# Returned rows read on the queue of the weights, the first tile behind the last weights; gate chunks split behind the last pair's scatters

## The chip, the cores and the metric

One core of a Trainium2 chip runs the kernel. The metric is the device time of one execution in microseconds (us). It has five engines that work side by side and wait for one another by semaphores: TensorE (PE in the profile; its weight loads are PEld), VectorE (DVE), ScalarE (ACT), GpSimd (POOL) and SyncE (SP). SP issues most DMAs here. DMAs issued by SP, ACT and POOL are carried out by the same 16 DMA engines.

## The reference, cut to what matters

One decoder layer over 512 tokens of width 1024, in float32. Everything up to the router is untouched; what counts here is the end of it.

```python
h = h + mix @ w_out
h = h + hier_moe(rmsnorm(h, norm2_g), ...)      # 32 gated-MLP experts, top 2 of one group
gate = sigmoid(rmsnorm(h, ple_norm_g) @ ple_gate_w + ple_gate_b)
e = p @ ple_proj_w
h = h + gate * e
return rmsnorm(h, final_norm_g)
```

## The kernel before, in words

**Experts.** The 32 experts run as 16 pairs (`for i in range(16)`, L1165). For a pair, `gate_up` (L991) multiplies 128 gathered rows (64 slots for each expert) by the gate and up weights, and `down` (L1014) by the down weights. The weights come as 96 units of 1 MB (`load_units`, L685) on SP, of which three are under way at a time: each waits for the one three before it. For pairs 0 to 14 the result is scattered to a table `yd` in device memory by an indirect DMA of POOL (L1043). The last pair doesn't go through memory: `down(15)` splits its result into a high part (`oh`, ACT, L1038) and a low part (`ol`, DVE, L1039), and `scatter` (L1046) adds it to the residual `h1` by matmuls with a one-hot matrix: two matmuls and one DVE addition for each of four token tiles and each half (hf) of the 1024 columns.

**Returned rows.** A tile t of 128 tokens gets back the two rows per token that the experts 0 to 14 of its choice left in `yd`: `load_y(t)` (L1160) reads them, 1 MB, into a buffer `ys[t]`, and `add_y(t)` (L1155) adds the two to `h1[t]`, one DVE instruction each. Since the rows come out of `yd`, the read must wait until the last scatter has landed. All four reads stand on POOL's queue, behind the last scatter.

**The gate matrix.** It comes in four loads of 1 MB (`gate_load`, L1058), on SP behind the last weights, then two rows of constants (`rows`). Each of its eight chunks k of 128 rows, in two halves of 512 columns, is split for the matmul (`split_gate`, L1062): ACT writes the rounded high part scaled by the norm's gain (L1068), DVE the low part (L1069). That makes 16 splits. In the code before, three stand in `down(15)` ahead of the high part of its result, one behind the first tile's scatters, and twelve behind `turn(0)`.

**The end.** `turn(t, hf)` (L1207) transposes half a tile on PE and copies it (ACT) and its rest (DVE). `ple(n)` (L739) runs n matmul steps of the embedding product `e` (PE, L724), which ACT takes out of PSUM (L735); the last twelve steps, three blocks of four, lie around the first tile's scatters and its `turn`. `rms(0)` (L1218) follows behind all splits and an activation table load (L1309). `tail` (L1266) then runs the four tiles: the 48 gate matmuls of each (L1234), its closing arithmetic (`finish`, L1236), and inside tile t the sums and the turn of tile t+1 (`sums`, L1278: `add_y` and two scatters).

On each engine this part of the program runs in the order in which it is written: PE, SP, ACT and DVE are under a manual schedule from pair 14 on, and POOL has little else to do.

PSUM banks go round by use (`Banks.USES`): "sc" has banks 4 and 5, "gu" banks 0 and 1, "pg" (the gate matmuls) banks 0 to 3. SBUF buffers of the name `unit` come from a ring: the first one freed is the next one used.

Of the kernel before, what the change touches and what calls it, by code (L numbers as in the profile page):

```python
# [17 lines left out]
P = 128  # L18
S = 512
D = 1024  # L20
NT = S // P
KC = D // P
# [16 lines left out]
def bcast(ap, parts=P):  # L39

    return bass.AP(tensor=ap.tensor, offset=ap.offset, ap=[[0, parts]] + [list(a) for a in ap.ap])
# [572 lines left out]
def ffn(ctx, tc, A, K, mixh, mixl, out, dbg, stage):  # L614

    nc = tc.nc
# [3 lines left out]
    dram, yd = K["dram"], K["yd"]  # L620
# [15 lines left out]
    def unit(dt, shape, slot=None):  # L636
        slot = slot or ring.pop(0)
        u = slot[0].tile(shape, dt, name="unit", tag=slot[1])
        slot_of[id(u)] = slot, u
        return u  # L640

    def free(*us):
        ring.extend(slot_of[id(u)][0] for u in us)

    def big(n, dt=F32, shape=(P, D)):
        return mw.tile(list(shape), dt, name="big", tag=f"big{n}")
# [20 lines left out]
    ps = K["ps"]  # L667
# [47 lines left out]
    def ple_steps():  # L715

        pT, pW = pl_in
        for j in range(8):
            t, hf = j // 2, j % 2
            p = ps("pe", "sc")  # L720
            for c in range(2):
                for k in range(2):
                    n = hf * 512 + c * 256
                    PE.matmul(p[:, c * 256:c * 256 + 256], pT[:, k * S + t * P:k * S + (t + 1) * P], pW[:, k, n:n + 256],  # L724
                              start=(k == 0), stop=(k == 1))
                    if c == k == 1:
                        kept.append((t, hf, p))
                        ple_out()
                    yield

    def ple_out():

        while kept and kept[0][0] // 2 < len(eo):
            t, hf, p = kept.pop(0)
            SC.activation(eo[t // 2][:, t % 2, hf * 512:hf * 512 + 512], p, AF.Copy)  # L735
# [3 lines left out]
    def ple(n):  # L739
        for _ in range(n):  # L740
            next(ple_left, None)
# [131 lines left out]
    with tc.manual_schedule(engines={mybir.EngineType.PE}):  # L873
        for hf in range(2):
            part(hf, 0, WO_LATE[:2])
        for n in range(len(halves) - 1):
# [5 lines left out]
            if n >= 2:  # L882
                t, hf = halves[n - 2]
# [130 lines left out]
    def down(i, behind=lambda n: None):  # L1014
        w, hid = hid_[i]
        pT = ps("ht", "ht")[:, :256].rearrange("p (f n) -> p f n", f=2)
        hT = mw.tile([P, 2, P], F32, name="hidT", tag="hidT")
        for f in range(2):
            PE.transpose(pT[:, f], hid[:, f * P:(f + 1) * P], ident)
        SC.activation(hT, pT, AF.Copy)  # L1020
        behind(0)
        o = out_[i] = []
        if i < 15:
            o = big(1)
        for hf in range(2):
            dn = ps("dn", "dn")
            for f in range(2):
                for e in range(2):
                    PE.matmul(dn[64 * e:64 * e + 64], hT[:, f, 64 * e:64 * e + 64],  # L1029
                              w[e][2][:, 1024 * f + 512 * hf:1024 * f + 512 * hf + 512],  # L1030
                              start=(f == 0), stop=(f == 1))
            if i < 15:
                SC.activation(o[:, 512 * hf:512 * hf + 512], dn, AF.Copy)  # L1033
                continue
            if hf == 0:
                o2 = unit(F32R, [P, 4, 512])
            oh, ol = o2[:, 2 * hf], o2[:, 2 * hf + 1]
            SC.activation(oh, dn, AF.Copy)  # L1038
            V.tensor_tensor(ol, dn, oh.bitcast(F32), ALU.subtract)  # L1039
            o.append((oh, ol))  # L1040
            behind(1 + hf)
        if i < 15:
            G.indirect_dma_start(out=yd, out_offset=bass.IndirectOffsetOnAxis(ap=idy[:, i:i + 1], axis=0), in_=o, in_offset=None,  # L1043
                                 bounds_check=2 * S - 1, oob_is_err=False)

    def scatter(j):  # L1046

        t, hf = j // 2, j % 2
        sc = ps("sc", "sc")
        for q in range(2):  # L1050
            PE.matmul(sc, DTs[15][:, t], out_[15][hf][q], start=(q == 0), stop=(q == 1))
        y = h1[t][:, 512 * hf:512 * hf + 512]
        V.tensor_tensor(y, y, sc, ALU.add)  # L1053


    gr, gw = [], {}

    def gate_load(j):  # L1058
        gr.append(unit(F32, [P, 4, 512]))
        nc.sync.dma_start(gr[j], A["ple_gate_w"][j])  # L1060

    def split_gate(k, hf):  # L1062

        if hf == 0:
            gw[k] = unit(F32R, [P, 2, D])
        hs = slice(hf * 512, hf * 512 + 512)
        raw, h, l = gr[2 * hf + k // 4][:, k % 4], gw[k][:, 0, hs], gw[k][:, 1, hs]
        SC.activation(h, raw, AF.Copy, scale=g3c[:, k:k + 1])  # L1068
        V.scalar_tensor_tensor(l, raw, g3c[:, k:k + 1], h.bitcast(F32), ALU.mult, ALU.subtract)  # L1069
        if k % 4 == 3:  # L1070
            free(gr[2 * hf + k // 4])
# [81 lines left out]
    ys = []  # L1153

    def add_y(t, rs=(0, 1)):  # L1155

        for r in rs:
            V.tensor_tensor(h1[t], h1[t], ys[t][:, r], ALU.add)  # L1158

    def load_y(t):  # L1160
        ys.append(unit(F32, [P, 2, D]))
        nc.gpsimd.dma_start(ys[t], yd.rearrange("(r n) d -> n r d", r=2)[t * P:(t + 1) * P])

    ends = ExitStack()
    for i in range(16):  # L1165
        if i == 14:
            ends.enter_context(tc.manual_schedule(engines={mybir.EngineType.Activation, mybir.EngineType.DVE}))
        gate_up(i, between(i))
        free(slab[6 * i + 1], slab[6 * i + 4])
        if i == 15:  # L1170
            break
        if i in (3, 7):
            eo.append(unit(F32, [P, 2, D]))
            ple_out()
        load_units()
        if i == 0:
            ple(PLE[0])
        gather_T(i + 1, 1)
        if i > 0:
            ple(PLE[i])  # L1180
        down(i, lambda n: gather_T(i + 1, 0))
        free(slab[6 * i + 2], slab[6 * i + 5])
        load_units()
        if i == 14:
            for t in range(NT):
                load_y(t)
            for j in range(4):
                gate_load(j)
            rows = mix.tile([P, 2, D], F32, name="rows", tag="m0")
            nc.sync.dma_start(rows[:, 0], bcast(A["ple_gate_b"]))  # L1190
            nc.sync.dma_start(rows[:, 1], bcast(A["final_norm_g"]))


    free(slab[92], slab[95])
# [85 lines left out]
        for hf in range(2):  # L1280
            scatter(2 * t + hf)

    def behind_down(n):
        if n == 0:
            for k in range(3):
                split_gate(k, 0)
            add_y(0, (0,))
        if n == 1:
            add_y(0, (1,))

    down(15, behind_down)
    ple(PLE_LAST[0])
    for hf in range(2):
        scatter(hf)
    split_gate(3, 0)
    ple(PLE_LAST[1])
    lo = [turn(0, hf) for hf in range(2)]
    ple(PLE_LAST[2])
    free(pl_in[1])
    for f in lo:  # L1300
        f()
    for k in range(4, KC):
        split_gate(k, 0)
    count_beyond()
    for k in range(KC):
        split_gate(k, 1)
    ov_slots = ring[:3]
    junk, h3s = (unit(F32, shape, slot) for shape, slot in zip(([P, 2, 512], [P, 4, 512]), ring[3:]))
    SC.preload_act_table_set("sigmoid_and_others")  # L1309
# [160 lines left out]
```

## Time and profile before

| | us |
|---|---|
| median of 3 runs (lowest, highest) | 566.47 (566.22, 566.54) |
| the profiled execution, its own time | 564.66 |
| span of the profiled execution, first to last instruction | 562.9 |
| around the span in that execution (564.66 - 562.9) | 1.76 |
| busy in the span: PE, DVE, ACT, POOL | 517.0, 276.7, 210.6, 90.3 |

All stretches below are given in us from the start of the span. The experts run from about 245 to 476; the change lies between the last weight load (463.6) and the first tile's end (about 506). A row of the chain of waits says what the last instruction's history was waiting for at each moment; "issue" there is time in which the engine waited for nothing that the profile shows.

### The profile page before, as it was taken

How to read it: one execution, taken by the hardware profiler on the slowest of the kernel's cores; microseconds unless marked ns; L12 is line 12 of the kernel's file. 1: busy time of each engine (PE TensorE's matmuls, PEld its weight loads, DVE VectorE, ACT ScalarE, POOL GpSimd, SP SyncE). 2: the span in 40 equal slices, each digit the busy share in tenths (PEclk: the TensorE clock that was granted, in tenths of full speed). 3: DMA queues.
4: the chain of work that ended last, by engine and by line, in shares of the span. 5: the costliest groups of instructions: out<-in, count | busy, mean ns of one | idle time of the engine just before them, and what ended most of it. 6: DMA issues, size and time to landing. Idle time of an engine off the chain costs nothing. (4 is left out here: it accounts for less than half of the span.)

```text
span 562.9 us, 7588 instructions
## 1 busy us (share of the span) xinstructions
PE 517.0 (92%) x2713; PEld 325.5 (58%) x2713; DVE 276.7 (49%) x735; ACT 210.6 (37%) x443; POOL 90.3 (16%) x126
## 2 busy tenths in 40 slices
PE   8999999999999999999999999988798897659992
PEld 5797886877996888853333333332223332448872
DVE  6663966847745667673222232221211112487764
ACT  7466765555856444211121111111011113173352
POOL 3301121311009300011111121100111002011110
PEclk9999999999999999999999999999999999788998
DMA  9881222300549589989999999999999999900111
GB/s 312 272 315 55 75 80 75 86 1 2 146 164 421 198 322 421 334 343 397 411 414 418 392 381 376 374 399 381 391 392 419 419 412 418 401 6 0 39 47 69
DMA packets 35641, 148.82 MB, mean 264 GB/s; under 512 B 6557, under 2 KB 14109, under 8 KB 22160
## 3 DMA queue, kind: packets, MB, share of 16 engines
q1 hardware_dynamic: 28896, 133.26, 61.8%
q0 software_dynamic: 5408, 12.15, 5.5%
q10 hardware_dynamic: 1296, 2.89, 1.3%
q8 instruction: 23, 0.38, 0.3%
q14 instruction: 18, 0.15, 0.1%
HBM read 139.61 MB, written 16.25 MB: 277 GB/s over the span
## 5 line engine op out<-in xcount | busy, mean ns | idle before, releaser
L997 PE MATMUL gu<-unit,xT 128*64 128x512 f32 x512 | 127.6, 598 | 12.4 <-DMA unit<-in_w_exp_dram 12.2
L997 PEld LDWEIGHTS gu<-unit,xT 128*64 128x64 f32 x512 | 37.1, 136 | 84.0 <-issue 59.0
L1029 PE MATMUL dn<-unit,hidT 128*64 128x512 f32 x256 | 61.0, 599 | 1.7 <-ACT hidT L1020 0.8
L234 PE MATMUL pj<-xh,wp 128*128 128x512 f32 x176 | 51.2, 398 | 0.4 <-ACT wp L69 0.4
L1234 PE MATMUL pg<-unit 128*128 128x512 f32 (+1 forms) x216 | 47.4, 376 | 1.1 <-ACT unit L1215 1.1
L1002 ACT ACTIVATE sg<-gu 128x256 f32<-128x256 f32 x16 | 6.2, 385 | 110.6 <-PE gu L997 110.6
L1003 DVE SCALAR_TENSOR_TENSOR hid<-sg,wsl,gu 128x256 f32<-128x256 f32 x16 | 7.7, 479 | 79.7 <-ACT sg L1002 79.7
L1234 PEld LDWEIGHTS pg<-unit 128*128 128x128 f32 x216 | 37.7, 192 | 9.0 <-ACT unit L1215 1.6
L1043 POOL DMA_INDIRECT yd<-big,idy x15 | 15.2, 1013 | 164.4 <-ACT big L1033 164.4
L1029 PEld LDWEIGHTS dn<-unit,hidT 128*64 128x64 f32 x256 | 19.1, 136 | 33.1 <-issue 24.5
L234 PEld LDWEIGHTS pj<-xh,wp 128*128 128x128 f32 x176 | 32.5, 188 | 8.0 <-ACT wp L69 1.1
L1033 ACT ACTIVATE big<-dn 128x512 f32<-128x512 f32 x30 | 17.9, 597 | 50.5 <-PE dn L1029 50.5
L930 DVE COPY SL<-sl 128x10 f32<-128x10 f32 (+1 forms) x17 | 2.9, 168 | 66.4 <-PE sl L929 66.4
L70 DVE TENSOR_TENSOR wp<-wraw,wp 128x768 fp32r<-128x768 f32 (+2 forms) x28 | 25.8, 928 | 13.7 <-ACT wp L69 13.4
L69 ACT ACTIVATE wp<-wraw 128x768 fp32r<-128x768 f32 (+2 forms) x28 | 22.8, 816 | 20.2 <-PE pj L234 9.8
L234 PE MATMUL pj<-xl,wp 128*128 128x512 f32 x88 | 29.4, 400 | 0.0
L986 DVE TENSOR_TENSOR xT<-xt,g2c 128x512 f32<-128x512 f32 x30 | 20.6, 688 | 11.8 <-PE xt L985 11.7
L80 PE MATMUL po<-wo,mx 128*128 128x512 f32 x96 | 25.7, 408 | 0.0
L257 PE MATMUL pj<-wp,xh 128*128 128x384 f32 x96 | 24.8, 351 | 0.0
L80 PE MATMUL po<-unit,mx 128*128 128x512 f32 x96 | 24.1, 399 | 0.0
L943 POOL DMA_INDIRECT xg<-tnd,idx x15 | 15.5, 1036 | 33.5 <-issue 15.8
L985 PEld LDWEIGHTS xt<-ident,xg 128*128 128x128 f32 x120 | 13.4, 140 | 11.5 <-issue 11.4
(294 smaller groups left out, 888.7 us busy)
## 6 DMA issues: line engine op xcount, KB each, us to landing
unit<-in_w_exp_dram SPq DMA_DIRECT2D x96, 1024.0 KB, 8.6
wraw<-in_w_in_dram SPq DMA_DIRECT2D x20, 384.0 KB, 3.5
yd<-zero SPq DMA_DIRECT2D x4, 1024.0 KB, 8.6
unit<-in_ple_gate_w_dram SPq DMA_DIRECT2D x4, 1024.0 KB, 15.0
unit<-yd POOLq DMA_DIRECT2D x4, 1024.0 KB, 19.3
wraw<-in_w_out_dram SPq DMA_DIRECT2D x8, 256.0 KB, 3.0
h<-in_x_dram SPq DMA_DIRECT2D x4, 512.0 KB, 5.2
unit<-in_w_out_dram SPq DMA_DIRECT2D x4, 512.0 KB, 9.2
```

What stands on the lines that cost most here:

```text
L69: nc.scalar.activation(h, src, AF.Copy)
L70: nc.vector.tensor_tensor(l, src, h.bitcast(F32), ALU.subtract)
L80: nc.tensor.matmul(p, a[k][:, ts_], K["wo"][k][:, b, hs], start=(n == 0), stop=(n == 3 * len(ks) - 1))
L234: PE.matmul(q, a[:, i * P:(i + 1) * P], b[k], start=(n == 0), stop=(n == 3 * KC - 1))
L257: PE.matmul(p[t][:, :W_IN[j]], a[k][:, t * P:(t + 1) * P], b, start=(n == 0), stop=(n == 3 * KC - 1))
L943: G.indirect_dma_start(out=xg[i % 2], out_offset=None, in_=tnd, in_offset=bass.IndirectOffsetOnAxis(ap=idx[:, i:i + 1], axis=0), bounds_ch ...
L986: V.tensor_tensor(xTs[i, hf], p.rearrange("p (a b) -> p a b", a=4), g2c[:, 4 * hf:4 * hf + 4, None].to_broadcast([P, 4, P]), ALU.mult)
L997: PE.matmul(gu[64 * e:64 * e + 64], xTs[i, k // 4][:, k % 4, 64 * e:64 * e + 64], w[e][k // 4][:, 512 * (k % 4):512 * (k % 4) + 512], star ...
L1029: PE.matmul(dn[64 * e:64 * e + 64], hT[:, f, 64 * e:64 * e + 64], w[e][2][:, 1024 * f + 512 * hf:1024 * f + 512 * hf + 512], start=(f == 0 ...
L1033: SC.activation(o[:, 512 * hf:512 * hf + 512], dn, AF.Copy)
L1043: G.indirect_dma_start(out=yd, out_offset=bass.IndirectOffsetOnAxis(ap=idy[:, i:i + 1], axis=0), in_=o, in_offset=None, bounds_check=2 * S ...
L1234: PE.matmul(p, hT[t][:, a, ks], gw[k][:, b, hs], start=start and n == 0, stop=stop and n == len(ab) - 1)
```

## The change

1. The four reads of returned rows go from POOL's queue to SP's. The first tile's stands directly behind the last weights and ahead of the four gate loads; the others lie between and behind the rows of constants.
2. `split_gate` becomes `gate_hi` (the ACT half) and `gate_lo` (the DVE half). None stands in `down(15)` any more. Two high parts (k = 0 and 1) and one low part stand around the first tile's scatters, and the rest behind `turn(0)`: 14 high parts and 15 low parts where 12 and 12 stood.
3. The products of the last three `ple` blocks (j of 5 and up) use the banks of "gu" instead of "sc".

```diff
-            p = ps("pe", "sc")
+            p = ps("pe", "sc" if j < 5 else "gu")
...
-    def split_gate(k, hf):
+    def gate_part(k, hf):
+        hs = slice(hf * 512, hf * 512 + 512)
+        return gr[2 * hf + k // 4][:, k % 4], gw[k][:, 0, hs], gw[k][:, 1, hs]
+
+    def gate_hi(k, hf):
 
         if hf == 0:
             gw[k] = unit(F32R, [P, 2, D])
-        hs = slice(hf * 512, hf * 512 + 512)
-        raw, h, l = gr[2 * hf + k // 4][:, k % 4], gw[k][:, 0, hs], gw[k][:, 1, hs]
+        raw, h, _ = gate_part(k, hf)
         SC.activation(h, raw, AF.Copy, scale=g3c[:, k:k + 1])
+
+    def gate_lo(k, hf):
+        raw, h, l = gate_part(k, hf)
         V.scalar_tensor_tensor(l, raw, g3c[:, k:k + 1], h.bitcast(F32), ALU.mult, ALU.subtract)
...
     def load_y(t):
         ys.append(unit(F32, [P, 2, D]))
-        nc.gpsimd.dma_start(ys[t], yd.rearrange("(r n) d -> n r d", r=2)[t * P:(t + 1) * P])
+        nc.sync.dma_start(ys[t], yd.rearrange("(r n) d -> n r d", r=2)[t * P:(t + 1) * P])
...
         if i == 14:
-            for t in range(NT):
-                load_y(t)
+            load_y(0)
             for j in range(4):
                 gate_load(j)
+            load_y(1)
             rows = mix.tile([P, 2, D], F32, name="rows", tag="m0")
             nc.sync.dma_start(rows[:, 0], bcast(A["ple_gate_b"]))
+            load_y(2)
             nc.sync.dma_start(rows[:, 1], bcast(A["final_norm_g"]))
+            load_y(3)
...
-    def behind_down(n):
-        if n == 0:
-            for k in range(3):
-                split_gate(k, 0)
-            add_y(0, (0,))
-        if n == 1:
-            add_y(0, (1,))
-
-    down(15, behind_down)
+    down(15, lambda n: n < 2 and add_y(0, (n,)))
     ple(PLE_LAST[0])
+    gate_hi(0, 0)
     for hf in range(2):
         scatter(hf)
-    split_gate(3, 0)
+    gate_lo(0, 0)
+    gate_hi(1, 0)
     ple(PLE_LAST[1])
     lo = [turn(0, hf) for hf in range(2)]
     ple(PLE_LAST[2])
     free(pl_in[1])
     for f in lo:
         f()
-    for k in range(4, KC):
-        split_gate(k, 0)
+    gate_lo(1, 0)
+    for k in range(2, KC):
+        gate_hi(k, 0)
+        gate_lo(k, 0)
     count_beyond()
     for k in range(KC):
-        split_gate(k, 1)
+        gate_hi(k, 1)
+        gate_lo(k, 1)
```

On SP, from the last weight load to the last load of all. unit_3823 is the last weight unit; before, this queue had only the gate matrix and the rows of constants behind it, and the four reads stood on POOL's:

```order
L691 DMA unit_3791<-in_w_exp_dram 128x2048
L691 DMA unit_3823<-in_w_exp_dram 128x2048
L1060 DMA unit_3948<-in_ple_gate_w_dram 128x2048
L1060 DMA unit_3950<-in_ple_gate_w_dram 128x2048
L1060 DMA unit_3952<-in_ple_gate_w_dram 128x2048
L1060 DMA unit_3954<-in_ple_gate_w_dram 128x2048
L1190 DMA rows_3956<-in_ple_gate_b_dram 128x1024
L1191 DMA rows_3956<-in_final_norm_g_dram 128x1024
```

After, in the same place:

```order
L691 DMA unit_3791<-in_w_exp_dram 128x2048
L691 DMA unit_3823<-in_w_exp_dram 128x2048
L1168 DMA unit_3940<-yd_73 128x2x1024
L1060 DMA unit_3942<-in_ple_gate_w_dram 128x2048
L1060 DMA unit_3944<-in_ple_gate_w_dram 128x2048
L1060 DMA unit_3946<-in_ple_gate_w_dram 128x2048
L1060 DMA unit_3948<-in_ple_gate_w_dram 128x2048
L1168 DMA unit_3950<-yd_73 128x2x1024
L1196 DMA rows_3952<-in_ple_gate_b_dram 128x1024
L1168 DMA unit_3954<-yd_73 128x2x1024
L1198 DMA rows_3952<-in_final_norm_g_dram 128x1024
L1168 DMA unit_3957<-yd_73 128x2x1024
```

The read of the first tile (unit_3940) now stands ahead of the four gate loads in one queue, and all that follows on SP is issued only when that read has been.

On ACT, from the last pair's transposed hidden rows (hidT) to the first splits behind the first tile's turn. dn is the last pair's result, pe a block of the embedding product, xt the transposed half tile; before:

```order
L1020 ACTIVATE hidT_4002<-ht_4001 128x256
L1068 ACTIVATE unit_4006<-unit_3948,g3c_1987 128x512
L1068 ACTIVATE unit_4009<-unit_3948,g3c_1987 128x512
L1068 ACTIVATE unit_4012<-unit_3948,g3c_1987 128x512
L1038 ACTIVATE unit_4021<-dn_4016 128x512
L1038 ACTIVATE unit_4021<-dn_4025 128x512
L735 ACTIVATE unit_3296<-pe_4032 128x512
L1068 ACTIVATE unit_4046<-unit_3948,g3c_1987 128x512
L735 ACTIVATE unit_3296<-pe_4049 128x512
L1215 ACTIVATE unit_4055<-xt_4056 128x512
L1215 ACTIVATE unit_4055<-xt_4062 128x512
L735 ACTIVATE unit_3296<-pe_4068 128x512
```

After, in the same place:

```order
L1020 ACTIVATE hidT_4002<-ht_4001 128x256
L1038 ACTIVATE unit_4012<-dn_4007 128x512
L1038 ACTIVATE unit_4012<-dn_4016 128x512
L735 ACTIVATE unit_3296<-pe_4023 128x512
L1071 ACTIVATE unit_4029<-unit_3942,g3c_1987 128x512
L1071 ACTIVATE unit_4040<-unit_3942,g3c_1987 128x512
L735 ACTIVATE unit_3296<-pe_4042 128x512
L1223 ACTIVATE unit_4048<-xt_4049 128x512
L1223 ACTIVATE unit_4048<-xt_4055 128x512
L735 ACTIVATE unit_3296<-pe_4061 128x512
L1071 ACTIVATE unit_4070<-unit_3942,g3c_1987 128x512
L1071 ACTIVATE unit_4073<-unit_3942,g3c_1987 128x512
```

The three high parts ahead of the last pair's result are gone; two stand between the first and the second block of the embedding product, and the row of splits behind the turn begins with k = 2 instead of k = 4. On PE the order is the same as before.

## Rows read from the trace of the kernel before

**Rows 1.** The chain of waits from the last scatter to the first tile's end, in order of time: start in us, length in us, what.

```profile
460.97 1.00 DMA yd<-big,idy
461.97 7.38 issue
469.35 0.02 POOLq L1162
469.37 12.27 DMA unit<-yd
...
481.69 1.11 issue
...
484.62 0.61 DVE unit L1039
...
492.73 7.46 ACT unit L1068 x12
...
500.20 1.28 ACT L1309
...
501.50 1.34 ACT unit L1221 x4
...
503.02 1.15 DVE h L1158
```

**Rows 2.** The same stretch on PE, instructions in order of time: start, length, engine, line, operation, output and inputs, shape, count, and in brackets the idle time before and who ended it.

```profile
472.32 3.65 PE L1029 MATMUL dn<-unit,hidT 128*64 128x512 f32 x16 [0.47 <-ACT hidT L1020]
475.91 1.99 PE L724 MATMUL pe<-unit,big 128*128 128x256 f32 x8
477.55 0.58 PE L1051 MATMUL sc<-unit,xT 128*128 128x512 f32 x1
483.54 1.22 PE L1051 MATMUL sc<-unit,xT 128*128 128x512 f32 x2 [5.41 <-DVE unit L1039]
485.27 0.80 PE L1051 MATMUL sc<-unit,xT 128*128 128x512 f32 x1 [0.51 <-DVE unit L1039]
485.87 3.73 PE L724 MATMUL pe<-unit,big 128*128 128x256 f32 x8
489.43 1.04 PE L1213 MATMUL xt<-ident,h 128*128 128x128 f32 x8
490.30 1.89 PE L724 MATMUL pe<-unit,big 128*128 128x256 f32 x8
...
492.22 4.42 PE L1234 MATMUL pg<-unit 128*128 128x512 f32 x18
496.48 1.08 PE L1051 MATMUL sc<-unit,xT 128*128 128x512 f32 x4
497.40 2.23 PE L1234 MATMUL pg<-unit 128*128 128x512 f32 x9
506.26 1.97 PE L1213 MATMUL xt<-ident,h 128*128 128x128 f32 x8 [6.63 <-DVE h L1053]
```

**Rows 3.** The same stretch on ACT, in order of time, columns as in rows 2.

```profile
476.12 1.06 ACT L1038 ACTIVATE unit<-dn 128x512 fp32r<-128x512 f32 x2
...
492.23 0.60 ACT L735 ACTIVATE unit<-pe 128x512 f32<-128x512 f32 x1 [1.03 <-PE pe L724]
```

**Rows 4.** The same stretch on DVE, in order of time, columns as in rows 2.

```profile
481.66 1.23 DVE L1158 TENSOR_TENSOR h<-h,unit 128x1024 f32<-128x1024 f32 x1 [4.56 <-DMA unit<-yd]
...
490.75 1.29 DVE L1216 TENSOR_TENSOR unit<-xt,unit 128x512 fp32r<-128x512 f32 x2 [3.29 <-ACT unit L1215]
...
496.20 5.37 DVE L1069 SCALAR_TENSOR_TENSOR unit<-unit,g3c 128x512 fp32r<-128x512 f32 x8
```

**Rows 5.** The stretches by window: start and end, length, busy time of PE, PEld, DVE, ACT and POOL with the instruction counts, granted TensorE clock (1.00 is full speed), DMA share, GB/s.

```profile
480.00:482.00 2.00, 0.00 (x0) 0.00 (x0) 0.34 (x1) 0.00 (x0) 0.00 (x0) 1.00 1.02 418
...
484.00:486.00 2.00, 1.49 (x4) 0.46 (x3) 1.81 (x3) 0.00 (x0) 0.00 (x0) 0.50 1.03 410
486.00:488.00 2.00, 2.00 (x6) 1.64 (x6) 1.35 (x2) 0.00 (x0) 0.00 (x0) 0.50 1.03 412
...
490.00:492.00 2.00, 2.00 (x13) 1.64 (x11) 1.25 (x2) 1.20 (x3) 0.00 (x0) 1.00 0.97 387
...
506.30:509.90 3.60, 3.60 (x13) 3.22 (x14) 2.78 (x5) 0.80 (x2) 0.00 (x0) 0.50 0.00 0
```

**Rows 6.** The last ten weight loads on SP, by source line, from 440 us on: durations of the issue in ns, first and last start in us.

```profile
L691 SPq DMA_DIRECT2D unit<-in_w_exp_dram x10: 327/328/328, 439.9 to 463.6; - x10
```

**Rows 7.** The DMA issues of the window from 463.0 to 463.9, which holds only the last weight load: tile, queue, count, size, time from issue to landing in us.

```profile
unit<-in_w_exp_dram SPq DMA_DIRECT2D x1, 1024.0 KB, 8.0
```

**Rows 8.** The four gate loads by source line, columns as in rows 6, and their times from issue to landing in us (lowest, median, highest).

```profile
L1060 SPq DMA_DIRECT2D unit<-in_ple_gate_w_dram x4: 442/484/539, 463.9 to 465.6; - x4
...
DMA to landing us min/median/max: 10.2/15.0/20.0
```

**Rows 9.** The four reads of returned rows by source line, columns as in rows 8.

```profile
L1162 POOL DMA_DIRECT2D unit<-yd x4: 716/729/772, 469.4 to 471.6; - x4
...
DMA to landing us min/median/max: 12.3/19.3/22.7
```

**Rows 10.** The fifteen scatters of POOL by source line, columns as in rows 8.

```profile
L1043 POOL DMA_INDIRECT yd<-big,idy x15: 997/1012/1024, 258.1 to 461.0; - x15
...
DMA to landing us min/median/max: 7.8/8.5/9.5
```

## The prediction, made before the changed kernel was run

> **What bounds the kernel now.** The chain of waits comes first [rows 1]. The last scatter is issued at 460.97, and POOL then stands until 469.35. The scatters take 7.8 to 9.5 us from issue to landing, the last one the lowest, 7.8 [rows 10], so it landed at about 468.8: POOL waited for exactly that. The first read of returned rows (y0 below) is issued at 469.37 and takes 12.27 us, to 481.64. From there the chain runs through the DVE additions, the scatter matmuls, the embedding blocks, the turn, then twelve ACT splits in a row (7.46), the table load, `rms(0)` and the second tile's `add_y` at 502.9 to 503.0.
>
> PE says what that costs [rows 2]. It has finished the last pair and the first embedding block at about 477.9, waits 5.41 us for DVE, and when it goes on its clock is low: 0.50 from 484 to 488, which is 1.2 GHz of 2.4, after a stretch without work around 480 to 482 in which the clock still read 1.00 [rows 5]. An embedding block takes 3.73 us there and 1.89 us later at full clock [rows 2]. DVE waited 4.56 us, put down to y0 [rows 4].
>
> Why y0 takes 12.27 us is seen in the loads. The last weight load is issued at 463.6 [rows 6] and lands 8.0 later, at 471.6 [rows 7]. The four gate loads are issued behind it at 463.9 to 465.6 and land 10.2 to 20.0 us after that, so the first at 474.1 and the last at 485.6 [rows 8]; the four y reads land 12.3 to 22.7 us after 469.4 to 471.6 [rows 9]. All of this shares 410 to 418 GB/s [rows 5]: 1 MB takes 1.049 / 0.418 = 2.5 us of it, and 474.1 - 471.6 is those 2.5. The first gate chunks are early, and y0, which PE waits for, is late.
>
> **The change part by part.** *y0's landing.* SP reaches y0 at 463.6 + 0.33 = 463.9 and stands until the last scatter has landed, 468.8 to 469.4. The last weights are then still on their way until 471.6. y0 takes the place behind them that the first gate load had, so I take that load's landing: 474.1, that is 7.5 earlier than 481.64. The near bound is 2.5 us behind the weights as well, or some tenths less if the weights leave room; the far bound is the row of before, 12.27 us after the issue, and no gain. I am near the first, since nothing is queued ahead of y0 then but the weights.
>
> A rule speaks on whether the queue itself does this. The rows show that y0 and the gate loads together moved at 410 to 418 GB/s, no less than one queue alone [rows 5]. The Trainium skill, "DMA: Bandwidth & Descriptors", section "Issuing engines are not separate DMA queues", says that DMAs from all issuing engines run on the same 16 DMA engines and interleave, and that issuing from another engine saves only sequencer time. By that rule the change of queue is worth nothing; only that the gate loads stand behind y0 is. A y0 on POOL that took turns with the gate loads would land one more MB later, at 476.6, and the sum would be about 2 us smaller; the trace agrees with it so far, as 481.64 is later still.
>
> *What is late next.* From y0's landing to the end of the second `ol` DVE needs 481.66 to 485.23 = 3.57 us, two additions and two low parts [rows 1, 4]. With 474.1 that ends at 477.7. ACT's `oh` no longer stands behind three splits, so both are there by about 476.6 (PE ends the last pair at 475.97 [rows 2], a copy takes 0.53 [rows 3]). PE reaches the first scatter matmul at 477.55 as before, and four take about 1.0 at full clock (496.48, next start 0.92 later [rows 2]). The fourth starts at 477.55 + 3 x 0.25 = 478.3, behind DVE's 477.7. So PE now sets the pace, y0 could land at 474.7 without cost, and beyond that each us costs one. There is no idle time on PE to lower its clock.
>
> *PE to the turn.* Scatters end at 478.5; the second embedding block takes 1.9 instead of 3.73 [rows 2]; the transposes start at 480.4 instead of 489.43: -9.0. From there to ACT's copy of the third block 489.43 to 492.23 = 2.8 us [rows 2, 3], so 483.2, still -9.0. The embedding products in other banks remove a possible wait of the second scatter for ACT, which the rows don't show, and add one: the gate products begin in the bank of the last block, so PE's first gate matmul waits for ACT's copy, 0.60 [rows 3]. It is hidden: PE waits 6.63 us later on for the second tile [rows 2].
>
> *The splits.* Twelve took 7.46 us, 0.62 each [rows 1]. Fourteen take 8.7. They start at 492.73 - 9.0 = 483.7 and end at 492.4 instead of 500.2: -9.0 + 1.24 = -7.8. The two high parts that stay ahead of the turn run while PE does scatters and the second block. DVE: eight low parts took 5.37 [rows 4], 0.67 each; fifteen take 10.1 from about 482.8 (the turn's low parts ended at 492.04 [rows 4], now 9.0 earlier, then one wait for ACT), so the last ends near 493.9, ahead of `rms(0)`'s result at 502.9 - 7.8 = 495.1. No cost.
>
> *Do the loads hold?* Behind y0 one MB each 2.5 us: gate loads at 476.6, 479.1, 481.6 and 484.1, y1 at 486.6, the constants and y2 by 491.7, y3 by 494.2. Needed: the first by ACT after the first block's copy, about 478.5; the others at 484.9, 487.4 and 489.9 (after 2, 6 and 10 of the 14 splits); y1 at 495.1; the constants near 499. The smallest cover is 1.9 us, the next 5.8.
>
> *Queues.* POOL loses four issues of 0.73 us [rows 9], for which nothing waited but y0. SP gains four of about 0.5 us, as the gate loads take [rows 8]; nothing but output stores stands behind them.
>
> *The end.* From the table load on nothing differs in order, so it moves as a whole. PE's wait for the second tile stays (about 8.5 us instead of 6.63), and the 3.6 us at clock 0.50 behind it [rows 5] should stay too.
>
> Sum against the profiled execution: 564.66 - 7.8 = 556.9. The median of the runs stands 1.81 above that execution, which I leave as it is: 566.47 - 7.8 = 558.7.
>
> **The rivals.** (a) *y0 is dragged by what stands behind it.* Its queue holds four gate loads right behind, and if their packets run beside y0's, it lands with the first of them at 476.6. DVE then ends at 480.2, 1.9 later than PE can use it: -5.9, 560.6. Against it: in the queue of before the loads land one after another at 2.5 us, in order of issue [rows 7, 8]. The Trainium skill, same page, section "Two DMAs through the same engine are not ordered", says that within a queue descriptors start in order but overlap, so an earlier one may finish its writes late; the rows so far bear out the start, and no row rules out the overlap.
>
> (b) *The gates come too late.* The first gate chunk now stands on ACT in front of the second block's copy and the turn. If the first gate load lands after about 480.2 instead of 476.6, ACT holds the turn; 2 us beyond that give -5.8, 560.7. Against: 3.6 us of cover up to there.
>
> (c) *SP stands too long.* All nine loads, gates included, now hang on one landing. The break-even is y0 at 474.7 + 7.8 = 482.5: the last scatter must land 8.4 later than here, 16 us after its issue. Its fifteen fellows took at most 9.5 [rows 10]. At 18 us the time would be 568.5, slower than before.
>
> (d) *It doesn't do what it says.* Another wait on y0's buffer holds SP; POOL's issue at 469.37 into the same buffer speaks against that. No change, 566.5.
>
> (e) *More.* If PE's clock didn't fall in the last gap, or the turn came earlier still, up to 1.5 more: 557.2.
>
> **How the numbers follow.** Forecast 0.66, (a) 0.14, (b) 0.07, (c) 0.04, (d) 0.03, (e) 0.06. About 0.2% (1.1 us) is what a measurement of this kernel can tell from no change. Faster: 0.66 + 0.14 + 0.07 + 0.06 = 0.93; within: 0.03; slower: 0.04. The range reaches from 557.0, near (e), to 561.4, past (a) and (b) with 0.7 for the spread of the runs, and leaves out (c) and (d).
>
> **What would show it.** Right: y0 issued on SP at 469 and landing near 474; PE's wait of 5.41 us gone and the clock at 1.00 through the second embedding block; the turn's transposes near 480.4; fourteen splits in a row from about 483.7; the second tile's `add_y` near 495; PE's second wait still there. Wrong: y0 landing past 474.7, a wait of ACT for a gate load ahead of the turn, or a tail longer than 562.9 - 502.9 = 60.0 us from that `add_y` on.

## The result, and the profile after

| | before | after |
|---|---|---|
| median of 4 runs in us (lowest, highest) | 566.35 (564.73, 566.54) | 557.63 (555.33, 559.88) |
| the profiled execution, its own time | 564.66 | 556.99 |
| its span | 562.9 | 555.2 |
| ratio after to before, with its 95% interval | | 0.9859 [0.9831, 0.9887] |

The kernel is 1.4% faster. The chain of waits of the changed kernel, from the last weights to the first tile's end (start in us, length in us, what), answers to [rows 1]:

```profile
457.86 9.15 DMA unit<-in_w_exp_dram
...
473.15 3.65 PE dn L1029 x16
476.81 1.93 PE pe L724 x8
478.73 0.93 PE sc L1051 x4
479.67 1.73 PE pe L724 x8
481.39 0.87 PE xt L1221 x8
482.27 1.74 PE pe L724 x8
...
484.52 8.68 ACT unit L1071 x14
...
496.05 1.15 DVE h L1164
```

The reader is to see what is gone: no read of returned rows (`unit<-yd`) and no DVE step between the last pair and the turn. PE runs from one block into the next. The same on PE, instructions in order of time, columns as in [rows 2], to which they answer:

```profile
473.15 3.65 PE L1029 MATMUL dn<-unit,hidT 128*64 128x512 f32 x16 [0.47 <-ACT hidT L1020]
476.74 2.00 PE L724 MATMUL pe<-unit,big 128*128 128x256 f32 x8
478.38 1.28 PE L1051 MATMUL sc<-unit,xT 128*128 128x512 f32 x4
479.50 1.89 PE L724 MATMUL pe<-unit,big 128*128 128x256 f32 x8
481.23 1.04 PE L1221 MATMUL xt<-ident,h 128*128 128x128 f32 x8
...
484.68 4.42 PE L1242 MATMUL pg<-unit 128*128 128x512 f32 x18 [0.59 <-ACT unit L735]
...
499.29 1.97 PE L1221 MATMUL xt<-ident,h 128*128 128x128 f32 x8 [7.18 <-DVE h L1053]
```

The waits of 5.41 and 0.51 are gone, and the second embedding block takes 1.89 instead of 3.73. The wait for the second tile is still there, 7.18. On SP, in order of time, and on DVE:

```profile
463.94 0.33 SPq L691 DMA_DIRECT2D unit<-in_w_exp_dram  x1
468.27 0.38 SPq L1168 DMA_DIRECT2D unit<-yd  x1
468.70 2.88 SPq L1060 DMA_DIRECT2D unit<-in_ple_gate_w_dram  x4
```

```profile
474.75 1.23 DVE L1164 TENSOR_TENSOR h<-h,unit 128x1024 f32<-128x1024 f32 x1 [2.57 <-DMA unit<-yd]
...
489.32 5.37 DVE L1075 SCALAR_TENSOR_TENSOR unit<-unit,g3c 128x512 fp32r<-128x512 f32 x8
...
495.96 2.48 DVE L1164 TENSOR_TENSOR h<-h,unit 128x1024 f32<-128x1024 f32 x2
```

SP stands 4.0 us behind the last weights, then issues y0 at 468.27, and DVE has it at 474.75, where [rows 4] has 481.66. By window, columns as in [rows 5]:

```profile
468.00:470.00 2.00, 2.00 (x12) 0.67 (x11) 0.59 (x2) 0.60 (x1) 0.00 (x0) 1.00 0.81 320
...
478.00:480.00 2.00, 2.00 (x11) 1.69 (x10) 1.06 (x3) 1.23 (x3) 0.00 (x0) 1.00 1.03 434
480.00:482.00 2.00, 2.00 (x15) 1.80 (x14) 1.19 (x2) 1.16 (x3) 0.00 (x0) 1.00 1.00 422
...
498.00:500.00 2.00, 0.71 (x4) 0.71 (x5) 1.90 (x4) 0.00 (x0) 0.00 (x0) 0.50 0.00 0
```

The granted clock is 1.00 through the scatters, the blocks and the turn; it falls to 0.50, the lower level, behind the wait for the second tile, as it did before [rows 5].

**Where the time came from**, by three marks: the start of the last pair's `dn`, the second tile's `add_y`, the end of the span.

| stretch | before | after | difference |
|---|---|---|---|
| start of the span to `dn` | 472.32 | 473.15 | +0.83 |
| `dn` to `add_y(1)` | 502.94 - 472.32 = 30.62 | 495.96 - 473.15 = 22.81 | -7.81 |
| `add_y(1)` to the end | 562.9 - 502.94 = 59.96 | 555.2 - 495.96 = 59.24 | -0.72 |
| sum | | | -7.7 |

The first line lies ahead of the work that the change moves: over the fourteen traces of this study `dn` starts anywhere from 470.99 to 476.31, behind the weights. So traces are compared from the start of `dn` below, and "from `dn`" is what is left of the span from there: 90.6 before, 82.05 after.

### The profile page after: what moved, and what is told of

Read it like the earlier page. It is cut to its first block, busy times and chain, and to the rows that moved or that the text cites. A ratio compares the mean times of both kernels' runs of the same rounds, so it can differ in the third digit from the quotient of the medians.

```text
span 555.2 us, 7581 instructions
## 1 busy us (share of the span) xinstructions
PE 514.5 (93%) x2713; PEld 325.3 (59%) x2713; DVE 276.2 (50%) x735; ACT 210.8 (38%) x443; POOL 87.1 (16%) x122
## 4 chain that ended last, share of the span: by engine, by line
PE 62%; DMA 18%; DVE 9%; ACT 7%; issue 2%; POOL 1%; SPq 0%; ACTq 0%; DVEq 0%; POOLq 0%
DMA unit<-in_w_exp_dram 17%; PE gu L997 12%; PE pj L234 9%; PE po L80 8%; PE dn L1029 7%; PE pj L257 5%; PE z L257 4%; PE z L311 2%; PE po L333 2%; PE pe L724 2%; ACT unit L1071 2%; PE x L974 1%; DVE h L1164 1%; PE pl L780 1%; PE z L292 1%
```

## The experiments

Each is an edit of the changed kernel. Ratios are to the kernel before, run on the same chip.

**1. The changed kernel again, beside 2 to 4.** No edit.

> The changed kernel as it is, again, as a reference for the runs beside it. Theory (the gain is y0 landing behind the last weights, 7.8 us less two more splits): 555 to 560 us, y0 landing at 474 to 476, no wait of PE between the last pair and the first scatter. Rival (the first run was a lucky one): over 561.

Measured: 556.8 against 565.16, 0.9852 [0.9798, 0.9906]; from `dn` 82.4. The first result holds. Here y0 was issued at 470.58, 2.3 later than in the first trace, and DVE had it 4.9 later, at 475.49, which is `dn` + 2.70, and PE's second embedding block starts 0.31 later behind `dn` than in the first trace. While SP stood, the queue ran empty (window, columns as in [rows 5]):

```profile
470.00:472.00 2.00, 0.94 (x5) 0.13 (x2) 0.88 (x3) 0.38 (x1) 0.00 (x0) 1.00 0.46 147
```

What the queue carried beside y0 differs too. In these traces the gate loads move in packets of 8 KB, the returned rows in packets of 4 KB. The packets of the window from 472.0 to 474.4, in the first trace and then in this one:

```profile
DMA packets 169, 1.00 MB, mean 416 GB/s; under 512 B 15, under 2 KB 15, under 8 KB 79
...
DMA packets 216, 0.88 MB, mean 369 GB/s; under 512 B 0, under 2 KB 0, under 8 KB 216
```

In the first trace 169 - 79 = 90 packets of the gate loads ran beside the last of y0's. Here all 216 are y0's.

**2. The reads alone.** SP's order and the banks as changed; the splits back in their old places.

```diff
...
-    down(15, lambda n: n < 2 and add_y(0, (n,)))
+    def behind_down(n):
+        if n == 0:
+            for k in range(3):
+                split_gate(k, 0)
+            add_y(0, (0,))
+        if n == 1:
+            add_y(0, (1,))
+
+    down(15, behind_down)
     ple(PLE_LAST[0])
-    gate_hi(0, 0)
     for hf in range(2):
         scatter(hf)
-    gate_lo(0, 0)
-    gate_hi(1, 0)
+    split_gate(3, 0)
...
```

The parts left out define `split_gate` again and put the other twelve splits back behind `turn(0)`.

> The new reads with the old places of the splits: three high parts stand again ahead of the last pair's result on ACT, with the first gate load now 2.5 us behind y0. Theory: ACT waits for that load until about 477.3, the result's high parts come 479.2 to 480.3, DVE ends its fourth step at 483.5 instead of 478.3, and twelve splits instead of fourteen give 1.2 back: 3 us above the changed kernel at full clock, 5 if the clock falls in PE's wait of about 4 us, so 560 to 562.5. Rival (the reads do it all and the splits' places are worth nothing): 1.2 below the changed kernel, 556.

Measured: 562.75 against 565.16, 0.9957 [0.9934, 0.9981]; from `dn` 87.5. On ACT and on PE, in order of time:

```profile
480.02 1.95 ACT L1071 ACTIVATE unit<-unit,g3c 128x512 fp32r<-128x512 f32 x3 [4.51 <-DMA unit<-in_ple_gate_w_dram]
```

```profile
482.50 0.49 PE L1051 MATMUL sc<-unit,xT 128*128 128x512 f32 x1 [1.36 <-ACT unit L1038]
484.64 1.22 PE L1051 MATMUL sc<-unit,xT 128*128 128x512 f32 x2 [1.65 <-DVE unit L1039]
486.38 0.80 PE L1051 MATMUL sc<-unit,xT 128*128 128x512 f32 x1 [0.51 <-DVE unit L1039]
486.97 3.54 PE L724 MATMUL pe<-unit,big 128*128 128x256 f32 x8
```

The wait moved from y0 to the first gate load: ACT stands 4.51 us for it, with the last pair's high part (L1038) queued behind three splits, and the clock falls as before (the block takes 3.54). So the reads alone bring 0.4% of the 1.4%. The time lies 0.25 above the range expected; the mechanism is the one expected, with the clock falling.

**3. The splits alone.** All four reads back on POOL; splits and banks as changed.

```diff
-        nc.sync.dma_start(ys[t], yd.rearrange("(r n) d -> n r d", r=2)[t * P:(t + 1) * P])
+        nc.gpsimd.dma_start(ys[t], yd.rearrange("(r n) d -> n r d", r=2)[t * P:(t + 1) * P])
...
-            load_y(0)
+            for t in range(NT):
+                load_y(t)
...
-            load_y(1)
...
-            load_y(2)
...
-            load_y(3)
```

> The new places of the splits and the new banks with the old reads on POOL. Theory: y0 lands at 481 to 482 as before, PE waits 5.4 us, and two more splits behind the turn cost 1.2: 567 to 568, slower than before. Rival (moving the splits out of the last pair's way is what freed PE): 558 to 560.

Measured: 566.68 against 565.16, 1.0018 [0.9997, 1.0039]; from `dn` 92.1, that is 1.5 more than before. On PE and on ACT:

```profile
482.74 1.22 PE L1051 MATMUL sc<-unit,xT 128*128 128x512 f32 x2 [5.94 <-DVE unit L1039]
...
492.03 8.69 ACT L1071 ACTIVATE unit<-unit,g3c 128x512 fp32r<-128x512 f32 x14
```

PE still waits for y0, and the row of fourteen splits takes 8.69 where twelve took 7.46. The runs can't tell this part from no change (the interval holds 1); in the trace it is a cost. It pays only with the reads.

**4. y0 behind the gate loads, on SP.**

```diff
-            load_y(0)
             for j in range(4):
                 gate_load(j)
+            load_y(0)
```

> All reads on SP as in the change, but the four gate loads stand ahead of y0. Theory (order, not queue): y0 lands behind four more MB at about 484, 2.5 us later than on POOL, and with two more splits the time is 3.7 above before: 569 to 571. Rival (a read on SP is quicker than one on POOL whatever its place): y0 by 476 and 557 to 560.

Measured: 568.45 against 565.16, 1.0062 [1.0037, 1.0088]; from `dn` 93.6.

```profile
486.56 1.22 PE L1051 MATMUL sc<-unit,xT 128*128 128x512 f32 x2 [8.07 <-DVE unit L1039]
```

SP's queue as such brings nothing. The same read on the same queue, four loads later, makes the kernel slower than before. DVE had y0 at 484.67, near the 484 expected; the time is half a us below the range.

**5. One gate load ahead of y0.**

```diff
+            gate_load(0)
             load_y(0)
-            for j in range(4):
+            for j in range(1, 4):
                 gate_load(j)
```

> The changed kernel with one gate load ahead of y0 on SP. Theory: y0 lands 2.5 us later, 476.8 to 477.4, DVE's fourth step ends 3.6 later, and PE's fourth scatter matmul is 1.3 to 2 us late: 1.5 to 2 above the changed kernel, with PE waiting there for DVE. Rival (there is more slack than reckoned): no wait of PE at the scatters, no difference.

Measured: 558.46 against 566.6, 0.9857 [0.9803, 0.9912]; from `dn` 84.2. On PE:

```profile
477.58 0.73 PE L1051 MATMUL sc<-unit,xT 128*128 128x512 f32 x2 [0.58 <-DVE unit L1039]
479.31 0.50 PE L1051 MATMUL sc<-unit,xT 128*128 128x512 f32 x1 [1.00 <-DVE unit L1039]
479.65 1.89 PE L724 MATMUL pe<-unit,big 128*128 128x256 f32 x8
```

y0 landed at 475.70, 4.51 behind `dn` (471.19), and the second block starts 2.1 later behind `dn` than in the first trace. The two short waits leave the clock at its higher level (the block takes 1.89). The run times don't show this cost: 0.9857 lies between the changed kernel's 0.9859 and 0.9852, and its interval spans 6 us. The cost is read from the traces, from `dn`: 84.2 against 82.05 and 82.4. With the other traces in which DVE has y0 early, these give what y0's landing is worth, in us behind `dn` (y0: when DVE begins to add it; experiment 9 is left out, as another wait stands there):

| trace | y0 | second embedding block starts | difference |
|---|---|---|---|
| the first trace | 1.60 | 6.35 | 4.75 |
| the changed kernel again (1) | 2.70 | 6.66 | 3.96 |
| second tile early, again (10) | 2.81 | 6.77 | 3.96 |
| second tile early (10) | 2.93 | 6.89 | 3.96 |
| gate loads behind y0, on POOL (8) | 3.06 | 7.01 | 3.95 |
| rows summed on POOL (11) | 3.67 | 7.63 | 3.96 |
| one gate load ahead (5) | 4.51 | 8.46 | 3.95 |

In six traces the block starts 3.95 to 3.96 behind y0: each us of y0 costs one there. In the first trace, the only one with y0 earlier than 6.35 - 3.96 = 2.4 behind `dn`, PE's own work sets the start.

**6. POOL's reads with the gate loads behind the scatter.** The reads go back to POOL; each gate load waits for the last scatter (`sent[-1]`), so that both queues start together.

```diff
...
-        nc.sync.dma_start(gr[j], A["ple_gate_w"][j])
+        got = nc.sync.dma_start(gr[j], A["ple_gate_w"][j]).ins
+        tc.add_manual_dep(got, sent[-1].name,
+                          mybir.DependencyInfo(mybir.DependencyClass.Sync, mybir.DependencyReason.DATA))
...
-        nc.sync.dma_start(ys[t], yd.rearrange("(r n) d -> n r d", r=2)[t * P:(t + 1) * P])
+        nc.gpsimd.dma_start(ys[t], yd.rearrange("(r n) d -> n r d", r=2)[t * P:(t + 1) * P])
```

> Reads on POOL as before, splits as in the change, and the four gate loads on SP wait for the last scatter too, so that y0 has no gate load ahead of it but takes turns with them. Theory (order is all, two queues take turns): y0 lands one MB later than in the changed kernel, at 476.5 to 477.5, and the time is 1.5 to 2 above it, 558.5 to 560. Rival one (POOL's queue is slow by itself): y0 at 480 or later, 564 to 567. Rival two (no turns, first come first served): y0 at 474.5 to 475, 557.

Measured: 567.1 against 566.6, 0.9998 [0.9974, 1.0023]; from `dn` 92.5. The theory that the two queues take turns, so that y0 lands one MB later, fell; the time is that of the rival by which POOL's queue is slow. POOL issued y0 at 471.03, 0.5 behind the first gate load on SP, and it took 12.9 us, to 483.93. The queues' rows (packets, MB, share of the 16 engines) of the window from 471 to 475, and then of 475 to 483:

```profile
q1 hardware_dynamic: 178, 1.29, 92.5%
...
q1 hardware_dynamic: 314, 2.29, 68.0%
q0 software_dynamic: 280, 1.10, 33.5%
```

q1 is SP's queue, q0 POOL's. For 4 us behind its issue POOL's queue moved nothing. Then the two moved about the same number of packets, but POOL's had 1.10 MB / 280 = 3.9 KB and SP's 7.3 KB, so that y0 had a third of the bytes. In the trace of before the windows read the same: y0 issued at 469.37, no packet of q0 up to 473, and from 473 to 481 284 packets with 1.11 MB against 306 with 2.24 MB.

**7. The same with y0 alone on POOL,** the other three reads on SP.

```diff
-        nc.gpsimd.dma_start(ys[t], yd.rearrange("(r n) d -> n r d", r=2)[t * P:(t + 1) * P])
+        (nc.gpsimd if t == 0 else nc.sync).dma_start(ys[t], yd.rearrange("(r n) d -> n r d", r=2)[t * P:(t + 1) * P])
```

> As the run with the reads on POOL and the gate loads held until the last scatter, but only y0 on POOL; the other three reads are on SP as in the change. Theory (the late start belongs to each read on POOL): first packets 4 us after the issue and y0 landing 12 to 13 us after it, 566 to 568. Rival (the four issues in a row, 2.9 us, are what delays the first): first packets 1 to 2 us after the issue, y0 landing 9 to 10 us after it, 563 to 565.

Measured: 566.99 against 566.1, 1.0009 [0.9986, 1.0033]; from `dn` 91.4. The issue on POOL, and the read's size and time from issue to landing:

```profile
473.19 0.77 POOL L1170 DMA_DIRECT2D unit<-yd  x1 [7.38 <-PE pD L1010]
...
unit<-yd POOLq DMA_DIRECT2D x1, 1024.0 KB, 13.0
```

No packet of q0 moved up to 477. Four issues in a row are thus not the cause of the late start, as the theory had said.

**8. POOL's reads with the gate loads behind y0.** As 6, but each gate load waits for y0's landing.

```diff
-        tc.add_manual_dep(got, sent[-1].name,
+        tc.add_manual_dep(got, yin[0].name,
...
```

The line left out keeps y0's read as `yin[0]`.

> Reads on POOL, splits as in the change, and the four gate loads on SP wait until y0 has landed, so that nothing shares with y0 once the weights are in. Theory (a read on POOL begins 4 us after its issue instead of 1.2, and beside gate loads gets a third of the bytes): alone it takes 4.1 + 2.5, so y0 lands 6.5 to 7 us after its issue, 2 us later than on SP; the first gate load then comes 4 to 6 us behind y0 and holds ACT ahead of the turn for 2 to 4 us. Time 560 to 563. Rival (a read on POOL moves slowly whatever is beside it): y0 lands 10 us or more after its issue, 566 or more.

Measured: 559.3 against 566.1, 0.9866 [0.9831, 0.9901]; from `dn` 86.2. POOL issued y0 at 469.96; DVE and ACT:

```profile
475.28 1.22 DVE L1166 TENSOR_TENSOR h<-h,unit 128x1024 f32<-128x1024 f32 x1 [4.02 <-DMA unit<-yd]
```

```profile
483.65 1.34 ACT L1073 ACTIVATE unit<-unit,g3c 128x512 fp32r<-128x512 f32 x2 [5.21 <-DMA unit<-in_ple_gate_w_dram]
...
491.01 5.06 ACT L1073 ACTIVATE unit<-unit,g3c 128x512 fp32r<-128x512 f32 x8 [0.42 <-DMA unit<-in_ple_gate_w_dram]
```

With only the other returned rows behind it, on its own queue, the read on POOL takes 5.3 us, against 4.9 on SP in experiment 1. So it isn't POOL's queue that makes y0 late, but what runs beside it. The theory, that a read on POOL always begins 4 us late, had y0 land 6.5 to 7 behind its issue; here its first packet moved 1.5 behind it, half a us after the last weight packet on SP's queue had begun (470.9). The run also shows the price of late gates: the first gate load, issued at 475.32, lands 8.3 later, the turn's copy on ACT stands behind it, and `add_y(1)` comes 26.6 behind `dn` instead of 22.81.

**9. The banks undone.**

```diff
-            p = ps("pe", "sc" if j < 5 else "gu")
+            p = ps("pe", "sc")
```

> The changed kernel with all embedding blocks in the banks of the scatters again. Theory (the banks are worth nothing here): the second half's scatter waits for ACT's copy of the first block, about 0.5 us, and the first gate matmul loses its wait of 0.6: within 0.7 us of the changed kernel. Rival (the banks are what keeps PE going): PE waits 2 us or more at the scatters, 559 or more.

Measured: 557.46 against 566.6, 0.985 [0.9791, 0.991]; from `dn` 82.6.

```profile
478.64 0.73 PE L1051 MATMUL sc<-unit,xT 128*128 128x512 f32 x2 [0.22 <-ACT unit L735]
479.21 1.99 PE L724 MATMUL pe<-unit,big 128*128 128x256 f32 x8
...
485.88 2.82 PE L1242 MATMUL pg<-unit 128*128 128x512 f32 x11 [0.17 <-DVE unit L1075]
```

The ratio can't be told from that of the changed kernel. In the trace the scatters now wait for ACT to empty the first embedding block, and the second block starts 6.84 behind `dn` instead of 6.35, although y0 was early (1.89). `add_y(1)` comes 23.4 behind `dn`, 0.6 later. One trace, and 0.1% of the time.

**10. The second tile ahead of the last splits.** `sums(1)` goes ahead of the second half's splits on DVE, the second tile's turn to the start of the first tile's second half (`at[1, 0]`), and the first tile's arithmetic behind both halves. Run twice, the second time beside 11.

```diff
+        for j, (hf, c, n, p) in enumerate(pieces if t == 0 else []):
+            first(j, p, slice(hf * 512 + c, hf * 512 + c + n))
...
-            first(j, p, hs)
+            if t > 0:
+                first(j, p, hs)
...
-                at[1, 1] = lambda: prep(t + 1)
-            if sums and t == 0:
-                at[0, 6] = lambda: sums(1)
+                at[1, 0 if t == 0 else 1] = lambda: prep(t + 1)
...
     count_beyond()
+    sums(1)
     for k in range(KC):
...
```

> The changed kernel, and the second tile's sums ahead of the second half's splits on DVE, its turn between the two halves of the first tile's gate products, and the first tile's closing arithmetic behind both halves. Theory (what is late next is the second tile's sums, queued on DVE behind fifteen low parts and the norm; PE waits 7.2 us for them and then runs 3.6 us at clock 0.50): the wait falls to 1 to 3 us, the clock stays at 1.00, and the time is 5 to 8 us below the changed kernel, 549 to 552. Rival (the tail is bound by DVE's own work): at most 2 us below, 555.

> The run with the second tile's sums early, again, beside the other one: 554 to 557.

Measured: 555.23 against 566.6, 0.9807 [0.9749, 0.9865], and 556.15 against 565.34, 0.9823 [0.9767, 0.9878]. From `dn` 80.8 and 80.7 against 82.05 and 82.4 of the changed kernel: 1.5 less. The intervals of the ratios overlap with the changed kernel's, so the gain rests on the traces. The theory's 5 to 8 us fell; the rival, at most 2, held. On PE, the first run and then the second:

```profile
491.39 1.25 PE L1221 MATMUL xt<-ident,h 128*128 128x128 f32 x8 [1.91 <-DVE h L1053]
...
515.73 4.71 PE L1242 MATMUL pg<-unit 128*128 128x512 f32 x12 [3.62 <-ACT unit L1223]
```

```profile
493.53 1.71 PE L1221 MATMUL xt<-ident,h 128*128 128x128 f32 x8 [1.90 <-DVE h L1053]
494.89 4.90 PE L1242 MATMUL pg<-unit 128*128 128x512 f32 x15
...
517.86 2.44 PE L1242 MATMUL pg<-unit 128*128 128x512 f32 x5 [2.10 <-ACT unit L1223]
```

PE's wait for the second tile fell from 7.18 to 1.9, but a new one came in front of a later tile. In the first run the clock stayed at 1.00 behind the wait of 1.91; in the second it was 0.51 in the window from 494 to 496, and PE lost about 1.5 there. Yet the later wait was 1.5 shorter, and the end the same. So PE doesn't set the tail's length then. DVE has no wait of more than 0.8 us from 485 to 516 in either trace, which points to DVE as what is late next; that is argued from its rows, not shown by a run.

**11. Rows of the last two tiles summed on POOL,** in addition to 10, to take work from DVE.

```diff
+        if t > 1:
+            V.tensor_tensor(h1[t], h1[t], ys[t][:, 0], ALU.add)
+            return
...
+    for t in range(2, NT):
+        G.tensor_tensor(ys[t][:, 0], ys[t][:, 0], ys[t][:, 1], ALU.add)
```

> The run with the second tile's sums early, and for the third and fourth tile the two returned rows are summed on POOL, so that DVE adds one row to h instead of two (the order of the additions differs, the sum is the same). Theory (with the second tile early, the tail is bound by DVE, whose 51 us of work and hand-overs with ACT fill it): DVE has 2 x 1.24 us less, and the time falls by 1 to 2.5 us against that run, 553 to 554.5. Rival (the tail is bound by PE's gate products or by the hand-overs alone): within 0.5 us.

Measured: 557.62 against 565.34, 0.9851 [0.9796, 0.9906]; from `dn` 83.4, 2.6 more than 10. The intervals of the ratios overlap, so this too rests on the traces. POOL and then DVE:

```profile
496.74 2.36 POOL L1314 TENSOR_TENSOR unit<-unit 128x1024 f32<-128x1024 f32 x1 [29.83 <-PE xt L1224]
500.54 2.67 POOL L1314 TENSOR_TENSOR unit<-unit 128x1024 f32<-128x1024 f32 x1 [1.44 <-DMA unit<-yd]
```

```profile
496.14 9.60 DVE L1075 SCALAR_TENSOR_TENSOR unit<-unit,g3c 128x512 fp32r<-128x512 f32 x8
```

The theory that it would gain 1 to 2.5 fell: eight low parts took 9.60 us on DVE beside the two POOL additions, 5.38 without them. That is 4.2 for 5.0 of POOL's work, more than the two additions taken from DVE (2 x 1.22) gave back: 4.2 - 2.4 = 1.8 of the 2.6. The other 0.8 is y0, which came that much later behind `dn` in this trace than in the two of 10 (table of experiment 5).

## Why the prediction was right

**The sum.** Predicted for the profiled execution 556.9, measured 556.99; for the median 558.7, measured 557.63. The 1.1 between the latter two is the one step that was left as it was: the median stood 1.81 above the profiled execution before, and 0.64 after. Inside the span three parts make the sum: -7.81 against -7.8 predicted, and +0.83 and -0.72, neither predicted, that cancel. The first of these is the weights' arrival. That they cancel is luck, and so is a forecast within 0.1 of one execution: the other three of the changed kernel lie 1.4 to 3.0 from 556.9. What the record bears out is the size, some 8 us, and the stretch where it arises.

**The tail.** It was said to move as a whole, 60.0 us long; it was 59.24. The row on PE that answers is the wait for the last tile's turn, 1.13 before and 0.23 after; why it shrank, no run here took apart.

**y0's landing: the forecast held, with luck; its mechanism only in part.** 474.1 was put at 2.5 us behind the last weights, in the first gate load's place; 474.73 was measured. The term that the prediction lacks is the read's own way from issue to landing. In five traces with y0 first on SP (experiments 1, 9, 10 twice, 11) SP was held by the scatter until at most 1.5 us ahead of the last weight packet, the queue ran low (147 GB/s in experiment 1), and DVE had y0 4.8 to 5.3 behind its issue: there it follows the scatter, not the weights. In the first trace the scatter landed early, at 468.2, and y0 was issued at 468.27 with weights still moving, their last packet at 471.2, much as the prediction had it. It then took 6.5, behind those weights and with gate packets beside it [experiment 1]. Which of the two costs how much of the 1.6 by which 6.5 exceeds 4.9, no run took apart. The limit, `dn` + 2.38 in the prediction's figures (474.7 - 472.32), measured as `dn` + 2.4; the slope beyond, one us for each, held to 0.01 us in six traces of the table. The prediction named a landing past 474.7 as a sign of being wrong, and 474.73 is past it by the letter; behind `dn`, which came 0.83 later, the first trace kept the limit with 0.8 to spare; of the others in this order on SP, one kept it and four passed it by 0.3 to 1.3.

**PE sets the pace; the clock.** Right in the first trace. The transposes start 8.08 behind `dn` instead of 17.11, so -9.03 for the predicted -9.0, and the clock is 1.00 up to the wait for the second tile.

**The splits.** 8.68 for the predicted 8.7, and the trace of experiment 3 shows what they cost without the gain. Their low parts end at 489.32 + 5.37 = 494.7, ahead of `add_y(1)`; no cost, as said.

**The banks.** The removed wait was counted at nothing, as the rows of before don't show it. With y0 early it is real: about 0.5 us on the path, in one trace [experiment 9]. The forecast held since the banks do change.

**PE's second wait.** Predicted 8.5, measured 7.18. The 0.60 by which PE starts the gate matmuls later has to be taken off this wait, not added: 6.63 + 1.24 - 0.60 = 7.27. It changed no time.

**POOL in turns with the gate loads.** The prediction let y0 on POOL land one more MB later and put the change of queue at about 2 us. This fell with experiment 6: the change of queue is worth all of it when gate loads run beside y0, since POOL's packets begin 4 us late and then get a third of the bytes; and it is worth some tenths when they don't [experiment 8]. The Trainium skill, "DMA: Bandwidth & Descriptors", section "Issuing engines are not separate DMA queues", by which another engine's queue saves only sequencer time, agrees with experiment 8 (5.3 us, against 4.9 on SP) and not with 6 and 7 (12.9 and 13.0). The Trainium skill, same page, section "Queues, rings and completion order", says that a DMA engine goes round its queues packet by packet; the counts of 314 and 280 agree with that, if a packet of the profile is what the skill calls one, which no run here shows. With like counts, the unequal sizes make the third.

**The rivals.** (a) The gates behind y0 did run beside its last packets in the first trace, and it landed 0.6 later than forecast; how much of that is theirs is open, and it cost nothing, as the limit was kept. In experiment 1 they did so only at the very end. (b) Late gates didn't occur; their price is real [experiment 8]: 3.8 us for a first gate load at 483.6, where the prediction's rule gives 483.6 - 480.2 = 3.4, and a second wait of ACT, for a later gate load, 0.42, makes up the rest. (c) SP stood 4.0 us; y0 was still in time. (d) is ruled out by the issue at 468.27. (e) The end could be better still [experiment 10], not by the clock but by the order of the second tile.

## What to carry to other kernels

A read that an engine waits for shares the DMA engines with everything already queued: what counts is which loads stand ahead of it and beside it, and a move of the read without a move of its neighbours (experiments 2 and 4) gave 0.4% or a loss. Before a load is moved forward, look up which engine's row of work waits for the loads that are thereby moved back, and move that work too. Work out the landing from which the time begins to depend on it; with that limit in hand a landing that is some tenths off costs what the slope says.

## What the runs showed of the hardware

- A read on POOL's queue beside gate loads on SP's queue moved its first packet 4 us after its issue (before, experiments 3, 6 and 7). With SP's queue out of loads it moved after 1.5 us (experiment 8). Why is open: it isn't the number of issues (7). A test with other loads on SP's queue wasn't made.
- 1 MB of returned rows on a queue that was running low was there 4.8 to 5.3 us after its issue from SP (five traces) and 5.3 from POOL (one), against 2.5 us for 1 MB in a full stream [rows 7, 8].
- Short waits of PE may or may not lower its clock: 0.58 and 1.00 left it at 1.00 (experiment 5); 1.91 left it there once, and after 1.90 it was 0.51 (experiment 10).
- Beside additions on POOL, DVE's low parts took 1.2 us each on average instead of 0.67 (experiment 11). The Trainium skill, "SBUF — State Buffer", section "Who interferes with whom", says that a DVE instruction with two inputs in SBUF contends with a GpSimd instruction that reads SBUF; the low part has two such inputs, and the 4.2 us lost beside 5.0 of POOL agree with it.
